# Four seams, an idle start and the last tile of a one-core decoder step: roundings put side by side, matmuls of ones, and a tile that ends in two parts

## The chip, the core and the metric

The kernel runs on one core of one Trainium2 chip. The metric is the device time of one execution in microseconds (us). TensorE (PE) multiplies matrices, VectorE (DVE) and ScalarE (ACT) work element by element on the memories SBUF and PSUM, GpSimd (POOL) gathers and raises to powers, SyncE (SP) issues transfers. Each engine runs its own instructions in the order in which they were written for it, and waits by semaphores for the others.

## The reference

One layer of a hybrid decoder runs for a prompt of 1024 tokens and, beside it, for eight tokens that are being sampled, each with a paged cache of 8192 positions. All numbers are float32.

```python
for l in range(DEPTH):                       # DEPTH = 1
    q, k, v, logf, u, z = mixer_inputs(rmsnorm(xp, g_mix[l]), w_in[l], ...)
    xp = xp + merge_heads(fox_prompt(q, k, v, logf), sgu_prompt(u, z, ...), ..., w_o[l])
    xp = xp + cross_attend(rmsnorm(xp, g_cross[l]), mk, mv, w_cq[l], w_co[l])
    f, conv_p = conv_ffn(rmsnorm(xp, g_ffn[l]), ..., w_up[l], conv_w[l], conv_b[l], w_down[l])
    xp = xp + f
    ...   # the same for the samples xs, with fox_sample over the paged cache
y_prompt = rmsnorm(xp, g_final)
y_sample = rmsnorm(xs, g_final)
```

`rmsnorm(x, g)` is `x * rsqrt(mean(x*x) + eps) * g` over the 1024 columns of a row. The model has 1024 columns, the gated MLP has 2 x 2816.

## The kernel before

**Numbers in two parts.** A float32 operand is split into a high part, rounded to the type fp32r by ACT (`h`), and a remainder `l = x - h` by DVE. A product is three matmuls into one PSUM bank: high times high, high times remainder, remainder times high (`gemm3`, L269 to L274). The weights go through the same split: `wr` is the raw weight, `wh` and `wl` its parts (L235 on ACT, L236 on DVE). `gemm3_late` (L276 to L284) multiplies all that needs only the high part of the rows first (L280, L281) and adds the products with the remainder at the end (L284).

**Stages.** The prompt goes in two halves of 512 rows (`hf` 0 and 1), each four tiles of 128 rows. Each half runs through the mixer, cross-attention and the MLP (`cross`, `ffn`). The samples run as a generator beside it (`decode`): gathers of cache pages by POOL (L1428 for keys, L1489 for values), products of keys and queries on DVE (L1444, in pairs), sums of them (L1448), and small matmuls on PE (L1495). Python code at the end of the kernel mixes the two by a table of costs (`PACE`), and a scheduler with a simulated time line then sets the order of the instructions of each engine. So an edit in one place can move rows of other places.

**A seam** is the change from one stage to the next (`norm_T`, L1106 to L1132). There are four: into cross-attention and into the MLP, for each half. The eight column blocks of the rows have to be transposed on PE, since the next products want columns on the partitions. Tiles 0 and 1 go first, then tiles 2 and 3. Each time four PSUM banks are filled, here called A, B, C and D, with two column blocks of 256 values each (L1124 writes them with four transposes). `split` then takes each block from the bank: ACT rounds it with its gain into `h` (L238), DVE writes the remainder `l` (L239). The two blocks of a bank lie in the same bank, and the program lets one engine at a time read a bank: ACT rounds block 0, DVE takes remainder 0, ACT rounds block 1, DVE takes remainder 1, and each step waits for the one before it. When all eight blocks of the first two tiles are there, `first` begins the next stage's first product with L280, L281 and L284, 256 columns wide.

In the seams into the MLP tiles 2 and 3 come late: `residual` adds the product's last part to the rows (L1015 on DVE) and squares them (L230 on ACT, which writes the row sums with a second instruction), `factor` makes the row's factor (L1031 on ACT, the power L1032 on POOL), and `both` scales tile 2 on ACT (L1044) and tile 3 on DVE (L1045) ahead of the transposes. Eight matmuls that compute nothing needed (`fill`, L1102) run there. In the seams into cross-attention the rows are transposed unscaled, so that only L1015 must be done.

**The start.** PE's first work is L306 (the samples' input product), then L479 to L481 (the prompt's); both wait for weights and rows from HBM. Before that DVE writes constants, `ones` (128x128) among them at L181.

**The end.** In the MLP's last group each tile's product is 15 matmuls of 512 columns, and `residual` follows. `final` (L1355 to L1363) makes the row factor of a tile from the two column halves' sums (L1020, L222 on DVE, the power L223 on POOL), multiplies the rows by factor and gain on DVE (L1361) and writes them with SP's queue (L1362), tile 3 in two halves.

## Time and profile before

| what | value |
|---|---|
| three timed runs | 1788.66, 1794.42 (median), 1794.93 us |
| the profiled execution | 1793.69 us, of which its span 1791.7 us |
| PE | 1735.9 us busy, 97% of the span |
| DVE | 1399.9 us, 78% |
| ACT | 733.5 us, 41% |
| POOL | 488.3 us, 27% |
| moved by DMA | 521.06 MB, mean 291 GB/s |

A row of the time line gives start, duration, engine, line of the kernel, operation, output and inputs by the program's names, shape, and in brackets how long the engine stood idle before it and which instruction ended that. Rows of PE are pipelined: a 512-column matmul's row is about 0.39 us long, while the next one starts 0.23 us after it. In a row of the waits stand the total, the number of times and the longest, in us. In a row of the stretches stand, for each engine, its busy time and its instructions, then the clock that PE was granted (1.00 is full), the DMA engines' share and GB/s.

### The profile page before, as it was taken

The numbers are of one execution on the slowest core, as the hardware profiler recorded it, in microseconds if no ns is written. First come the engines' busy times: TensorE is split into PE (matmuls) and PEld (weight loads), VectorE is DVE, ScalarE is ACT, GpSimd is POOL, SyncE is SP. The second block draws the span as 40 slices with busy tenths as digits, with TensorE's granted clock in tenths as the row PEclk, the third lists the DMA queues.
The fourth block names the chain that finished last, engine by engine and source line by source line (L and its number), as shares of the span: only waits on it lengthen the run. The fifth ranks groups of instructions, "written<-read, shape, count | busy, mean of one in ns | idle before, by whom it ended". The sixth has DMA issues, their size and how long they took to land.

```text
span 1791.7 us, 25124 instructions
## 1 busy us (share of the span) xinstructions
PE 1735.9 (97%) x9653; PEld 1285.7 (72%) x9653; DVE 1399.9 (78%) x1733; ACT 733.5 (41%) x1374; POOL 488.3 (27%) x461
## 2 busy tenths in 40 slices
PE   8999999889999999999999999999999999999997
PEld 5787777655677666767777777766666778768875
DVE  4689658989788986989999999898885549855344
ACT  6332355566643635333333244335353233333232
POOL 1252234443222332333322223433322112102110
PEclk9999999999999999999999999999999999999999
DMA  8786798777697975779788788988879587568982
GB/s 291 297 304 226 294 334 319 259 264 244 254 403 279 363 299 224 282 285 345 290 301 313 291 317 311 376 306 346 320 280 350 214 306 249 191 260 297 359 310 80
DMA packets 157074, 521.06 MB, mean 291 GB/s; under 512 B 20874, under 2 KB 40842, under 8 KB 124186
## 3 DMA queue, kind: packets, MB, share of 16 engines
q0 software_dynamic: 57168, 341.14, 50.0%
q1 hardware_dynamic: 92874, 165.73, 26.5%
q10 hardware_dynamic: 6912, 12.59, 1.9%
q8 instruction: 76, 1.25, 0.3%
q14 instruction: 44, 0.36, 0.1%
HBM read 495.47 MB, written 23.93 MB: 290 GB/s over the span
## 4 chain that ended last, share of the span: by engine, by line
PE 53%; issue 9%; DMA 8%; DVE 6%; ACT 2%; POOL 2%; POOLq 0%; DVEq 0%; ACTq 0%; SPq 0%
DMA kv<-cache_v,io 6%; PE ba L272 6%; PE ba L274 6%; PE ba L273 6%; PE dv L1495 4%; PE bb L272 3%; PE bb L273 3%; PE bb L274 3%; PE ba L1063 1%; DVE s L1448 1%; PE ba L1064 1%; PE ba L1065 1%; PE dv L331 1%; DMA kv<-cache_k,io 1%; PE dv L1774 1%
## 5 line engine op out<-in xcount | busy, mean ns | idle before, releaser
L235 ACT ACTIVATE wh<-wr 128x1024 fp32r<-128x1024 f32 (+2 forms) x220 | 228.6, 1044 | 443.3 <-PE ba L273 142.3
L236 DVE TENSOR_TENSOR wl<-wr,wh 128x1024 fp32r<-128x1024 f32 (+2 forms) x220 | 262.7, 1200 | 165.1 <-PE ba L274 57.4
L1428 POOL DMA_INDIRECT kv<-cache_k,io x128 | 186.9, 1460 | 606.8 <-DVE s L1448 327.2
L1444 DVE TENSOR_TENSOR kv<-kv,d 128x1024 f32<-128x1024 f32 (+1 forms) x156 | 258.0, 1681 | 32.6 <-DMA kv<-cache_k,io 32.6
L1448 DVE TENSOR_REDUCE s<-kv 128x16 f32<-128x1024 f32 (+1 forms) x156 | 258.4, 1672 | 0.0
L1489 POOL DMA_INDIRECT kv<-cache_v,io x128 | 160.8, 1256 | 239.4 <-PE dv L1495 155.2
L272 PE MATMUL ba<-u,wh 128*128 128x512 f32 x528 | 209.3, 397 | 0.0
L274 PE MATMUL ba<-u,wl 128*128 128x512 f32 x528 | 209.0, 396 | 0.0
L273 PE MATMUL ba<-u,wh 128*128 128x512 f32 x528 | 208.5, 395 | 0.5 <-DVE u L239 0.5
L272 PE MATMUL ba<-wh,u 128*128 128x512 f32 (+1 forms) x495 | 186.1, 379 | 0.9 <-ACT u L235 0.9
L273 PE MATMUL ba<-wl,u 128*128 128x512 f32 (+1 forms) x495 | 185.1, 375 | 1.3 <-DVE wl L236 1.3
L274 PE MATMUL ba<-wh,u 128*128 128x512 f32 (+1 forms) x495 | 183.4, 375 | 0.0
L1495 PE MATMUL dv<-kv,s 128*32 128x512 f32 x1024 | 127.1, 598 | 1.6 <-DMA kv<-cache_v,io 1.6
L274 PEld LDWEIGHTS ba<-u,wl 128*128 128x128 f32 x528 | 99.2, 188 | 29.0 <-issue 6.5
L272 PEld LDWEIGHTS ba<-u,wh 128*128 128x128 f32 x528 | 99.3, 188 | 26.4 <-issue 4.8
L273 PEld LDWEIGHTS ba<-u,wh 128*128 128x128 f32 x528 | 99.2, 188 | 25.2 <-issue 2.3
L272 PEld LDWEIGHTS ba<-wh,u 128*128 128x128 f32 x495 | 93.0, 188 | 25.0 <-issue 6.5
L272 PE MATMUL bb<-u,wh 128*128 128x512 f32 x272 | 108.7, 400 | 0.0
L274 PE MATMUL bb<-u,wl 128*128 128x512 f32 x272 | 108.0, 398 | 0.0
L273 PE MATMUL bb<-u,wh 128*128 128x512 f32 x272 | 107.9, 397 | 0.0
L273 PEld LDWEIGHTS ba<-wl,u 128*128 128x128 f32 x495 | 93.0, 188 | 20.1 <-DVE wl L236 1.9
L274 PEld LDWEIGHTS ba<-wh,u 128*128 128x128 f32 x495 | 92.9, 188 | 19.5 <-issue 1.6
(454 smaller groups left out, 3310.6 us busy)
## 6 DMA issues: line engine op xcount, KB each, us to landing
wr<-w_up SPq DMA_DIRECT2D x88, 512.0 KB
kv<-w_up POOLq DMA_DIRECT2D x22, 1024.0 KB
wr<-w_down SPq DMA_DIRECT2D x40, 512.0 KB
kv<-w_down POOLq DMA_DIRECT2D x11, 1024.0 KB
wr<-w_in SPq DMA_DIRECT2D x16, 512.0 KB
wr<-w_o SPq DMA_DIRECT2D x16, 512.0 KB
wr<-w_cq SPq DMA_DIRECT2D x16, 512.0 KB
wr<-w_co SPq DMA_DIRECT2D x16, 512.0 KB
```

What stands on the lines that cost most here:

```text
L235: nc.scalar.activation(h, src, AF.Copy)
L236: nc.vector.tensor_tensor(l, src, h.bitcast(F32), op=ALU.subtract)
L272: mmul(out, sh, mh, start=(i == 0), stop=False)
L273: mmul(out, sh, ml, start=False, stop=False)
L274: mmul(out, sl, mh, start=False, stop=(i == n - 1))
L331: mmul(ps[32 * j : 32 * j + 32, :w], xT[:, k, :] if nk == 8 else xT[:, k * 8 : k * 8 + 32], raw[:, q, j * w : (j + 1) * w], start=(k == 0) ...
L1063: mmul(pss[i], mh[k][:, tb], wh, start=(k == korder[0]), stop=False)
L1428: nc.gpsimd.indirect_dma_start(kv, None, a["cache_k"], off(kidx[:, b, ch : ch + 1]))
L1444: nc.vector.tensor_tensor(kvv[:, i : i + m, :], kvv[:, i : i + m, :], qb.unsqueeze(1).broadcast_to((P, m, 512)), op=ALU.mult)
L1448: nc.vector.tensor_reduce(s[:, ch * 4 + i : ch * 4 + i + m, :].rearrange("p k h -> p (k h)"), kvv[:, i : i + m, :].rearrange("p k (h d) -> ...
L1489: nc.gpsimd.indirect_dma_start(kv, None, a["cache_v"], off(kidx[:, b, ch : ch + 1]))
L1495: mmul(dv[32 * j : 32 * j + 32, :], s[:, ch * 4 : ch * 4 + 4, :].rearrange("p k h -> p (k h)"), kvv[:, j, :], start=(ch == 1), stop=(ch == ...
```

## The change

It has three parts. In `norm_T` ACT now rounds both blocks of a bank one after the other (L1133), and DVE takes both remainders after that (L1135). At the start thirteen matmuls of `ones` by `ones` go into a PSUM tile that nothing reads. The last tile (`last_tile`) is multiplied in two column halves of 256 columns; each half is added (L1311), squared, and its sum taken into the row's mean by ACT (L1313), so that the factor is there after POOL's power (L1316); and `final` multiplies the first 512 columns of tiles 2 and 3 by the gain early (L1398 on DVE), scales them by the factor on ACT (L1399) and writes them apart, tile 3's by ACT's queue (L1400), while DVE does the other 512 columns (L1395).

```diff
+    wm = MS()
+    for _ in range(13):
+        mmul(wm[:, :P], ones, ones, start=True, stop=True)
...
-                    for q in range(2):
-                        k = kk + q
-                        split(tr[:, q * 256 : (q + 1) * 256], hs[k][:, c], ls[k][:, c], scale=gp[:, g0 + k : g0 + k + 1])
+                    gain = [gp[:, g0 + k : g0 + k + 1] for k in (kk, kk + 1)]
+                    src = [tr[:, q * 256 : (q + 1) * 256] for q in range(2)]
+                    for q in range(2):
+                        nc.scalar.activation(hs[kk + q][:, c], src[q], AF.Copy, scale=gain[q])
+                    for q in range(2):
+                        nc.vector.scalar_tensor_tensor(
+                            ls[kk + q][:, c], src[q], gain[q], hs[kk + q][:, c].bitcast(F32), op0=ALU.mult, op1=ALU.subtract
+                        )
...
+        def last_tile(x, sq, pairs):
+            c2 = sm([P, 2], "lsq", 1)
+            part = sm([P, 2], "lpart", 1)
+            r3 = sm([P, 1], "lr", 1)
+            nc.scalar.activation(part[:, 0:1], sq[:, 3, 0:1], AF.Identity, scale=1.0 / D, bias=epsb)
+            for m in range(2):
+                ps = MM()
+                c = slice(m * 256, m * 256 + 256)
+                gemm3(ps[:, :256], [(sh, sl, mh[:, c], ml[:, c]) for sh, sl, mh, ml in pairs])
+                xs_ = x[:, 512 + m * 256 : 768 + m * 256]
+                with tc.high_priority():
+                    nc.vector.tensor_tensor(xs_, ps[:, :256], xs_, op=ALU.add)
+                    ssq_into(c2[:, m : m + 1], xs_)
+                    nc.scalar.activation(
+                        r3 if m else part[:, 1:2], c2[:, m : m + 1], AF.Identity, scale=1.0 / D, bias=part[:, m : m + 1]
+                    )
+            nc.gpsimd.tensor_tensor(r3, r3, mhalf[:, 0:1], op=ALU.pow)
+            lastr.append(r3)
...
+                    if hf and n and i == 3 and f0 + gn == NF:
+                        last_tile(xt[3], sq, [(gh[k][:, tb], gl[k][:, tb], ws[k][0], ws[k][1]) for k in range(gn)])
+                        continue
...
+            if hf and i > 1:
+                r = lastr[0] if i == 3 else rows_rstd(sq, i, i + 1)
+                for n, c in enumerate((slice(0, 512), slice(512, D))):
+                    if n:
+                        nc.vector.scalar_tensor_tensor(xt[i][:, c], xt[i][:, c], r, gf[:, c], op0=ALU.mult, op1=ALU.mult)
+                        nc.sync.dma_start(a["o_y"][rows, c], xt[i][:, c])
+                    else:
+                        nc.vector.tensor_tensor(xt[i][:, c], xt[i][:, c], gf[:, c], op=ALU.mult)
+                        nc.scalar.activation(xt[i][:, c], xt[i][:, c], AF.Copy, scale=r)
+                        (nc.scalar if i == 3 else nc.sync).dma_start(a["o_y"][rows, c], xt[i][:, c])
+                continue
```

The new lines move the old ones down by 3, and by 8, 29, 32 and 44 further on: L238 is now L241 in `split`'s scaled form (the seams no longer use it), L1124 is L1127, L1015 is L1018, L280, L281 and L284 are L283, L284 and L287, L230 is L233, L235 and L236 are L238 and L239, L1444 and L1448 are L1488 and L1492.

Of the order of the instructions three places are shown. The first is ACT at the seam into the MLP of the second half. `u` on the left of a row is the `h` being written, `ba` or `bb` the PSUM bank that it is taken from, `junk` the target of a square, `fac` a row factor. Before:

```order
L238 ACTIVATE u_11036<-ba_11038,gp 128x256 [waits PE_49]
L238 ACTIVATE u_11047<-bb_11049,gp 128x256 [waits PE_49]
L238 ACTIVATE u_11058<-ba_11060,gp 128x256
L238 ACTIVATE u_11036<-ba_11038,gp 128x256 [waits DVE_49]
L238 ACTIVATE u_11069<-ba_11071,gp 128x256
L238 ACTIVATE u_11047<-bb_11049,gp 128x256 [waits DVE_49]
L238 ACTIVATE u_11058<-ba_11060,gp 128x256 [waits DVE_49]
L238 ACTIVATE u_11069<-ba_11071,gp 128x256 [waits DVE_49]
L235 ACTIVATE wh_11391<-wr_11388 128x1024 [waits DMAHW5_49,PE_49]
L230 ACTIVATE junk_11018,sqx_10655<-u_9515 128x512 [waits DVE_49]
L1031 ACTIVATE fac_2074_11023<-sqx_10655,part_10656 128x1 [waits Activation_49]
```

and of the change:

```order
L233 ACTIVATE junk_11032,sqx_10669<-u_9529 128x512 [waits DVE_49]
L1034 ACTIVATE fac_2075_11037<-sqx_10669,part_10670 128x1 [waits Activation_49]
L1133 ACTIVATE u_11050<-ba_11052,gp 128x256 [waits PE_49]
L1133 ACTIVATE u_11050<-ba_11052,gp 128x256
L1133 ACTIVATE u_11061<-bb_11063,gp 128x256 [waits PE_49]
L1133 ACTIVATE u_11061<-bb_11063,gp 128x256
L238 ACTIVATE wh_11405<-wr_11402 128x1024 [waits DMAHW5_49,PE_49]
L1133 ACTIVATE u_11072<-ba_11074,gp 128x256 x2
L1133 ACTIVATE u_11083<-ba_11085,gp 128x256 x2
L233 ACTIVATE junk_11035,sqx_10669<-u_9531 128x512 [waits DVE_49]
L1047 ACTIVATE u_11118<-u_9529,fac_2075_11037 128x512 [waits Pool_49]
```

The waits of ACT for DVE inside the banks are gone; tile 2's square and its factor, which stood behind all eight roundings, now stand ahead of them, and a weight's rounding stands between banks B and C.

The second place is DVE at the seam into cross-attention of the second half, from bank D on. `u_9515` and `u_9517` (now `u_9529` and `u_9531`) are tiles 2 and 3, `kv` the samples' keys, `s` their scores. Before:

```order
L239 SCALAR_TENSOR_TENSOR u_9943<-ba_9944,gp,u_9942 128x256 [waits DMAHW5_49,DMAHW4_49,Activation_49]
L1444 TENSOR_TENSOR kv_9600<-kv_9600,d_1632_8613 128x1024 [waits DMASW5_49]
L1444 TENSOR_TENSOR kv_9600<-kv_9600,d_1632_8613 128x1024
L1015 TENSOR_TENSOR u_9515<-ba_9800,u_9515 128x512 [waits PE_49]
L239 SCALAR_TENSOR_TENSOR u_9943<-ba_9944,gp,u_9942 128x256 [waits Activation_49]
L236 TENSOR_TENSOR wl_9904<-wr_9902,wh_9905 128x1024 [waits DMAHW7_49,PE_49]
L1015 TENSOR_TENSOR u_9517<-ba_9801,u_9517 128x512 [waits PE_49]
```

and of the change:

```order
L1135 SCALAR_TENSOR_TENSOR u_9957<-ba_9958,gp,u_9956 128x256 [waits Activation_49]
L1135 SCALAR_TENSOR_TENSOR u_9957<-ba_9958,gp,u_9956 128x256
L1488 TENSOR_TENSOR kv_9614<-kv_9614,d_1633_8627 128x1024 [waits DMASW5_49]
L1488 TENSOR_TENSOR kv_9614<-kv_9614,d_1633_8627 128x1024
L1492 TENSOR_REDUCE s_8629<-kv_9614 128x16 [waits DVE_49]
L1488 TENSOR_TENSOR kv_9664<-kv_9664,d_1633_8627 128x1024 [waits DMASW6_49]
L1488 TENSOR_TENSOR kv_9664<-kv_9664,d_1633_8627 128x1024
L1018 TENSOR_TENSOR u_9529<-ba_9814,u_9529 128x512 [waits PE_49]
L239 TENSOR_TENSOR wl_9918<-wr_9916,wh_9919 128x1024 [waits DMAHW7_49,PE_49,Activation_49]
L1492 TENSOR_REDUCE s_8629<-kv_9614 128x16 [waits DVE_49]
L1018 TENSOR_TENSOR u_9531<-ba_9815,u_9531 128x512 [waits PE_49]
```

The two remainders now stand together, and tile 2's addition has moved behind a sum and a second pair of key products, tile 3's behind one more sum.

The third place is DVE at the end of the program, from the last product of tile 2 on. `rn2r` and `rn3r` are the factors of tiles 2 and 3 (tile 3's is now `lr`), the last operand of L1361 and L1395 is the gain. Before:

```order
L222 TENSOR_SCALAR rn2r_14800<-rq_2654_14798 128x1 [waits DVE_49]
L1361 SCALAR_TENSOR_TENSOR u_9515<-u_9515,rn2r_14800,u_14782 128x1024 [waits Pool_49]
L1015 TENSOR_TENSOR u_9517<-bb_14762,u_9517 128x512 [waits PE_49]
L1020 TENSOR_TENSOR rq_2656_14805<-sqx_11184 128x1 [waits Activation_49]
L222 TENSOR_SCALAR rn3r_14807<-rq_2656_14805 128x1 [waits DVE_49]
L1361 SCALAR_TENSOR_TENSOR u_9517<-u_9517,rn3r_14807,u_14782 128x512 [waits Pool_49]
```

and of the change:

```order
L1311 TENSOR_TENSOR u_9531<-bb_14780,u_9531 128x256 [waits PE_49]
L225 TENSOR_SCALAR rn2r_14840<-rq_2660_14838 128x1 [waits DVE_49]
L1395 SCALAR_TENSOR_TENSOR u_9529<-u_9529,rn2r_14840,u_14822 128x512 [waits Pool_49]
L1311 TENSOR_TENSOR u_9531<-ba_14800,u_9531 128x256 [waits PE_49]
L1395 SCALAR_TENSOR_TENSOR u_9531<-u_9531,lr_14778,u_14822 128x512 [waits Pool_49]
```

The last tile's addition is in two, its sums are off DVE, and tile 2's scaling on DVE is half as wide.

More of the change, by code (lines that the diff above doesn't have):

```diff
@@ L1357, in final @@
         for i in range(4):
+            rows = slice((hf * 4 + i) * P, (hf * 4 + i + 1) * P)
+            if hf and i > 1:
[9 more added lines that the diff above has]
+                continue
             r = rows_rstd(sq, i, i + 1)
-            rows = slice((hf * 4 + i) * P, (hf * 4 + i + 1) * P)
             for c in (slice(0, 512), slice(512, D)) if i == 3 else (slice(0, D),):
@@ L1365, in build @@
     lastexp = []
+    lastr = []
     last = {}
```

## The prediction

> **What bounds the kernel now.** I read the busy times first, then the waits, and last the time line and the stretches at the places that the change touches.
>
> ```profile
> PE 1735.9 (97%) x9653; PEld 1285.7 (72%) x9653; DVE 1399.9 (78%) x1733; ACT 733.5 (41%) x1374; POOL 488.3 (27%) x461
> ACT u L238 <- DVE u L239: 11.7, 7, 3.7
> ```
>
> TensorE is busy for 97% of the span of 1791.7 us. All its idle time is 1791.7 - 1735.9 = 56 us, and part of that lies at the two ends and in stages that no edit touches. So nothing here can win more than some ten microseconds. The last row is what the first edit aims at: ACT waits 11.7 us in seven places for a remainder. That is ACT's time. What counts is how much of it TensorE waits too.
>
> **The end.**
>
> ```profile
> 1781.75 1.28 DVE L1361 SCALAR_TENSOR_TENSOR u<-u,rn2r,u 128x1024 f32<-128x1024 f32 x1 [0.65 <-POOL rn2r L223]
> 1782.00 0.40 PE L274 MATMUL bb<-wh,u 128*128 128x512 f32 x1
> 1782.95 0.68 DVE L1015 TENSOR_TENSOR u<-bb,u 128x512 f32<-128x512 f32 x1
> 1783.73 0.63 ACT L230 ACTIVATE junk<-u 128x512 bf16<-128x512 f32 x1 [3.26 <-DVE u L1015]
> 1784.27 0.19 ACT L230 ACTIVATION_READ_ACCUMULATOR junk<-u 128x1 f32 x1
> 1784.91 0.54 POOL L223 TENSOR_TENSOR rn3r<-rn3r,mhalf 128x1 f32<-128x1 f32 x1 [3.20 <-DVE rn3r L222]
> 1785.49 1.42 DVE L1361 SCALAR_TENSOR_TENSOR u<-u,rn3r,u 128x512 f32<-128x512 f32 x2 [0.66 <-POOL rn3r L223]
> ```
>
> For the new widths I take rows of the seams, 256 columns on DVE and on ACT, and ACT's sum of one column:
>
> ```profile
> 698.53 0.28 ACT L1031 ACTIVATE fac<-sqx,part 128x1 f32<-128x1 f32 x1
> 1178.49 0.47 DVE L239 SCALAR_TENSOR_TENSOR u<-bb,gp,u 128x256 fp32r<-128x256 f32 x1
> 1178.99 0.47 ACT L238 ACTIVATE u<-bb,gp 128x256 fp32r<-128x256 f32 x1 [2.19 <-DVE u L239]
> ```
>
> TensorE ends at 1782.40 and DVE's last scaling at 1786.91. In the change TensorE ends 0.1 later (thirty narrow matmuls for fifteen). Tile 2's scaling on DVE takes 0.71 in place of 1.28 and ends as TensorE does. Then: second addition 0.47 (a 256-wide row) to 1783.0, square 0.47 + 0.19 to 1783.65, sum by ACT 0.28, POOL 0.54 to 1784.6, and ACT's scaling 0.63 beside DVE's 0.71: 1785.3. That is 1.6 us earlier. The last two transfers now start together, from SP's and from ACT's queue, behind which nothing stands any more; before, 0.7 us lay between them, so sharing costs between nothing and 0.7: I take 0.3. **-1.3** (bounds -1.6 and -0.9). The early multiplications by the gain stand ahead of a weight's remainder some 15 us before the end; if that has no slack, each costs its 0.7 us.
>
> **The seams.** In each bank DVE's first remainder now waits for two roundings, 0.47 more, and the weights' remainders and key products behind it on DVE with it; ACT's second rounding waits for nothing. There are four seams. At the first one (517 to 545 us) TensorE has no gap over 0.6 us; I count 0. The second, into the MLP of half 0:
>
> ```profile
> 696.32 1.33 ACT L1044 ACTIVATE u<-u,fac 128x512 f32<-128x512 f32 x2 [0.68 <-POOL fac L1032]
> 697.71 0.33 PE L1124 MATMUL bb<-cp,u 128*128 128x128 f32 x1 [1.70 <-ACT u L1044]
> 698.17 0.45 ACT L238 ACTIVATE u<-bb,gp 128x256 fp32r<-128x256 f32 x1
> 698.68 0.39 PE L280 MATMUL ba<-u,wh 128*128 128x256 f32 x1 [0.64 <-ACT u L238]
> 700.77 1.84 PE L1102 MATMUL ba<-u 128*128 128x256 f32 x7
> 704.07 0.38 PE L280 MATMUL ba<-u,wh 128*128 128x256 f32 x1
> ```
>
> Bank D's second rounding (698.17) stands behind tile 2's scaling and tile 3's square on ACT, so TensorE waits 1.70 and 0.64 us. In the new order both roundings of D stand ahead of tile 2's square, and L283, L284 and most of L287 run some 3 us earlier. But the path that ends this seam is tile 2's and tile 3's: addition, square, factor, scaling, transposes. On DVE three more remainders now stand ahead of tile 2's addition (3 x 0.47, by the row of 1178.49), so scaled tile 2 comes 1.2 us later, and tile 3's scaling is moved back as far. Against that stands the clock:
>
> ```profile
> 696.16:699.57 3.41, 1.22 (x8) 1.03 (x9) 0.59 (x2) 3.22 (x9) 0.67 (x2) 1.00 1.03 429
> 699.58:702.98 3.40, 3.40 (x18) 3.40 (x17) 2.27 (x7) 0.60 (x2) 1.01 (x1) 0.50 0.64 266
> ```
>
> In the first stretch TensorE was busy for 1.22 of 3.41 us; in the next it was granted half its clock, and the fill and the transposes took twice their time, about 1.7 us more. With the work before the scaling moved into that first stretch TensorE would be busy there for over 2 us, and the half clock may not come. 1.7 less what the later scaling takes: I count **-1.0** (bounds: -3.0 if both waits and the half clock go, +0.6 if the scaling is late and the half clock stays).
>
> The Trainium skill ("TensorE: Matmul & The Clock Gate", section "HAM oscillation — how this bites in real kernels") states the rule as no idle gaps over about 3.4 us. This trace differs: the longest gap here was 1.70 us and the clock fell all the same, with 36% of the stretch busy. By the page's rule the clock could not be at stake at this seam.
>
> The third seam, into cross-attention of half 1:
>
> ```profile
> 1168.58 2.35 DVE L1444 TENSOR_TENSOR kv<-kv,d 128x1024 f32<-128x1024 f32 x2
> 1170.85 0.68 DVE L1015 TENSOR_TENSOR u<-ba,u 128x512 f32<-128x512 f32 x1
> 1171.84 1.22 DVE L236 TENSOR_TENSOR wl<-wr,wh 128x1024 fp32r<-128x1024 f32 x1
> 1172.97 0.69 DVE L1015 TENSOR_TENSOR u<-ba,u 128x512 f32<-128x512 f32 x1
> 1173.57 2.33 DVE L1448 TENSOR_REDUCE s<-kv 128x16 f32<-128x1024 f32 x2
> 1176.21 2.35 DVE L1444 TENSOR_TENSOR kv<-kv,d 128x1024 f32<-128x1024 f32 x2
> 1176.35 0.50 PE L273 MATMUL ba<-u,wh 128*128 128x512 f32 x1 [0.47 <-DVE u L239]
> 1179.52 0.39 PE L280 MATMUL bb<-u,wh 128*128 128x256 f32 x1 [1.70 <-ACT u L238]
> ```
>
> Here the edit fits best. The remainder of 1178.49 stands behind a pair of key products (2.35), ACT's rounding of 1178.99 waits 2.19 for it and TensorE 1.70, with 0.47 before: 2.2 us go if nothing takes their place. Something does. In the new order of DVE tile 2's addition stands behind pair, sum and pair, 2.35 + 1.17 + 2.35 = 5.9 us after D's remainders where it was 2.35, and tile 3's behind an addition, a weight's remainder and one more sum: 0.69 + 1.22 + 1.17. Bank D's transposes have moved up to bank C's in the new order of TensorE, so I let DVE begin the pair 1.1 us earlier, at 1167.5 (my estimate). Tile 2's addition then ends at 1174.1 (before: 1171.5) and tile 3's at 1177.2 (before: 1173.7). By my count of the products ahead of them TensorE comes to tile 2's transposes at about 1171.2 and stands for 2.9 us, does nineteen products of 256 columns (2.3 us) and stands for 0.7 us more: 3.6 in place of 2.2, a loss of 1.4. The walk holds only if DVE is as far behind as before. Between -2.2 and +1.4 I take **0**.
>
> The fourth, into the MLP of half 1:
>
> ```profile
> 1322.01 0.47 ACT L238 ACTIVATE u<-ba,gp 128x256 fp32r<-128x256 f32 x1 [1.10 <-PE ba L1124]
> 1322.98 0.68 DVE L1460 TENSOR_TENSOR s<-s,dec 128x512 f32<-128x512 f32 x1
> 1325.23 0.84 ACT L238 ACTIVATE u<-ba,gp 128x256 fp32r<-128x256 f32 x2 [2.02 <-DVE u L239]
> 1326.43 0.39 PE L280 MATMUL ba<-u,wh 128*128 128x256 f32 x1 [1.05 <-DVE u L239]
> 1327.17 1.05 ACT L235 ACTIVATE wh<-wr 128x1024 fp32r<-128x1024 f32 x1
> 1329.84 1.34 ACT L1044 ACTIVATE u<-u,fac 128x512 f32<-128x512 f32 x2 [0.68 <-POOL fac L1032]
> 1330.61 0.33 PE L1124 MATMUL ba<-cp,u 128*128 128x128 f32 x1 [0.77 <-ACT u L1044]
> ```
>
> ACT's 2.02 and TensorE's 1.05 look like the same gain again. But the new order puts tile 2's square ahead of bank A's roundings, and that waits for tile 2's addition, which waits for DVE to end L1460 (1323.66). Addition 0.68, square 0.63 + 0.19, factor 0.28: A's first rounding starts at 1325.5 where it was 1322.01, and TensorE's first product at 1326.0 instead of 1326.43. Eight roundings at 0.42 and the weight's 1.05 between B and C end at 1329.9, then tile 3's square (0.82) stands ahead of tile 2's scaling: 1330.7 instead of 1329.84. Tile 3's scaling comes out as before. One wait gives way to another: **0** (bounds -2.5, with all the gaps from 1326 to 1333.4 gone, and +0.8).
>
> **The start.**
>
> ```profile
> 0.83 0.17 DVE L181 MEMSET ones<- 128x128 f32 x1 [0.83 <-PEq L2010]
> 7.15 1.92 PE L306 MATMUL ba<-wr,xg 128*32 128x512 f32 x4 [7.15 <-DVE u L239]
> 9.00 0.80 PE L479 MATMUL bb<-wh,u 128*128 128x512 f32 x1
> 10.29 0.40 PE L479 MATMUL bb<-wh,u 128*128 128x512 f32 x1
> ...
> 700.49 0.63 PE L1124 MATMUL ba<-cp,u 128*128 128x128 f32 x2
> ```
>
> TensorE does nothing until 7.15, and L479 took 0.80 us at 9.00 and 0.40 at 10.29: the clock doubled in between. The ones hide wholly in the idle 7 us, so they cost nothing, and delay nothing since the tile is read by nobody. They gain if they bring the full clock earlier, at most half of the 3.0 us from 7.15 to 10.1. Two f32 products of 128 columns took 0.63 us at the half clock, so thirteen end by 1.1 + 13 x 0.32 = 5.2 at the latest, and at least 2 idle us follow. By the second seam's rows a stretch with so little work in it gives the half clock back. I count **-0.1** (bounds: -0.9, half of L306's 1.92 us, and +0.5 if the clock's stretches fall worse).
>
> The Trainium skill (the same page, "Part 1: The HAM clock gate") holds that the full clock comes after a busy window of about 3.4 us and goes after an idle one. By that rule too thirteen matmuls are too few and too early, as an estimate; no run here shows it yet.
>
> **Sum.** -1.0 + 0 + 0 - 0.1 - 1.3 = -2.4 us, against the profiled execution's 1793.69 us: 1791.3 us. That execution is 0.73 us below the median of 1794.42; I leave it at that, since single runs lie 6 us apart. The order moves in most other stages as well: about 1,000 of some 7,000 rows of TensorE stand elsewhere. Their waits can fall either way; from the two 1.7 us gaps above I allow 4 us to each side.
>
> **Rivals.** (1) *The seams give all they show.* DVE is less far behind than in my walk: -3.0 - 2.2 - 2.5 at the seams, -0.5 at the start, -1.5 at the end, 9.7 us together: 1784.0. For it: two waits of ACT of 2 us each with TensorE idle behind them, and a stretch at half the clock. Against it: the new orders of ACT and DVE.
> (2) *Slower.* At the third seam the second pair of key products decides. If TensorE reaches tile 2's transposes before that pair ends, it stands for 3.6 us within 6, under half busy as in the stretch ahead of 699.58, and one or two stretches at half the clock follow, 1.7 us each. With 2 x 1.7 + 1.4 there, +0.8 and +0.6 at the other two, and 1.3 gained at the end, it is +4.9: 1798.6. It decides from the point where tile 2's addition comes over 3 us later than it did.
> (3) *The seams do nothing*, since a TensorE that is 97% busy takes the work up later: only the end's gain is left, 1792.4, and the other rows' moves around it.
>
> **Chances.** My sum 0.40, with a range of its own from 1787 to 1795; (1) 0.25; (2) 0.16; (3) 0.15; the rest (the other stages' order moves more than 4 us) 0.04. The range from 1780 to 1799.5 takes in (1) with its 4 us below, (2) at its price, and leaves out the far ends of both. Half a per cent is 9 us, about what a measurement of this kernel can tell from no change. Faster by more (under 1785.4) is the larger part of (1) and a little of the rest: 0.22. Slower by more (over 1803.4) is the far end of (2): 0.05. Within: 0.73.
>
> **What would show it.** In the profile after: L1133 without a wait for L1135 at all four seams; at 700 us the fill's seven matmuls in under 1 us if the clock held; TensorE's gap ahead of L1127 at the third seam (2.9 us by my walk), and ACT's first L1133 at the fourth at about 1325.5 rather than 1322; L309 still at 1.9 us; DVE's last L1395 some 2.9 us after TensorE's last matmul, where it was 4.5. I am wrong if L309 takes about 1 us and the program moves forward with it, if the third seam has no gap over 1 us, or if the waits of stages without an edit change by more than the seams do.

## The result and the profile after

The change takes 1803.22 us (median of 8 executions, 1799.53 to 1810.58), the kernel before beside it 1794.07 us (8 executions, 1788.66 to 1795.85). The ratio is 1.0060, with a 95% interval from 1.0041 to 1.0078: slower. The profiled execution of the change took 1803.68 us, of which its span is 1801.9 us, 10.2 us more than the span before. First the row of busy times:

```profile
PE 1744.2 (97%) x9694; PEld 1292.4 (72%) x9694; DVE 1398.0 (78%) x1733; ACT 732.5 (41%) x1381; POOL 490.2 (27%) x461
```

TensorE is busy for 8.3 us more than before and idle for 57.7 us in place of 55.8. The start shows why these two do not tell the story yet:

```profile
1.05 5.46 PE L188 MATMUL ms<-ones 128*128 128x128 f32 x26 [1.05 <-DVE mhalf L183]
7.14 1.05 PE L309 MATMUL ba<-wr,xg 128*32 128x512 f32 x4 [0.63 <-DVE u L242]
8.14 0.50 PE L482 MATMUL bb<-wh,u 128*128 128x512 f32 x1
```

The ones are 5.46 us of new "work" in time that was idle. Without them TensorE's busy time is 1738.7, 2.8 us more than before. Its idle time, without the first 7 us, has grown from 48.6 (55.8 - 7.15) to 56.0 (57.7 - 1.05 - 0.63): 7.4 us. These two are the loss. The busy part fits the clock: between the start and the end the trace grants TensorE half its clock for 17.1 us before (five stretches of 3.41 us) and for 23.9 us after (seven), which costs at most half of the difference, 3.4 us. To find the loss's place I cut both traces at the same rounding instructions of the prompt's weights, and compare the lengths (us):

| stretch before | what runs there | before | after | difference | the same order in other kernels |
|---|---|---|---|---|---|
| 0 to 71.3 | start, input products | 71.31 | 69.41 | -1.90 | -1.4 to -0.8 |
| 689.8 to 716.0 | second seam | 26.25 | 22.96 | -3.29 | 0.0 to +1.0 |
| 1164.7 to 1198.2 | third seam | 33.42 | 35.14 | +1.72 | 0.0 to +1.5 |
| 1319.9 to 1347.4 | fourth seam | 27.58 | 28.09 | +0.51 | -1.2 to -1.0 |
| 1766.4 to the end | last tile | 25.29 | 24.37 | -0.92 | 0.0 to +0.2 |
| 309.0 to 490.1 | attention, half 0 | 181.11 | 184.12 | +3.01 | -2.3 to +0.1 |
| 538.0 to 644.9 | end of the first seam, cross-attention, half 0 | 106.88 | 110.67 | +3.79 | +0.4 to +3.7 |
| 1052.5 to 1164.7 | mixer's end and merge, half 1 | 112.26 | 119.77 | +7.51 | -0.3 to +1.4 |
| 1198.2 to 1319.9 | cross-attention, half 1 | 121.70 | 118.43 | -3.27 | -1.1 to +5.9 |
| the five others | | 1085.9 | 1088.9 | +3.03 | -0.5 to +1.3 |

The last column says how far one execution can be trusted. It has the differences from before in kernels of the next section that leave TensorE's order in that stretch as it was before (the last tile alone, four ones, narrow ones, the first seam alone; each left out where its own edit lies). The second seam and the stretches of 309 and 1052 us stand clear of it, those of 538 and 1198 us do not. The first five rows, where the edits are (bar the first seam, which a cut divides), gain 3.9 us together. The others lose 14.1. (Work moves across the cuts too, so that one row is not idle time alone; the sum is the span's 10.2.) Three stretches before, by engine:

```profile
537.98:644.86 106.88, 104.74 (x536) 74.87 (x536) 93.70 (x119) 52.41 (x121) 29.08 (x25) 1.00 0.84 315
689.75:716.00 26.25, 22.82 (x131) 18.63 (x134) 17.20 (x31) 14.93 (x32) 3.06 (x4) 0.93 0.63 252
1102.30:1127.50 25.20, 24.41 (x127) 18.57 (x126) 23.78 (x30) 13.55 (x26) 11.71 (x9) 1.00 0.96 364
```

and the same three after:

```profile
540.22:650.89 110.67, 107.08 (x535) 76.50 (x534) 92.98 (x117) 51.40 (x122) 33.48 (x25) 0.97 0.80 298
695.78:718.74 22.96, 20.05 (x119) 16.91 (x117) 14.73 (x30) 12.26 (x28) 3.06 (x4) 1.00 0.72 288
1108.40:1137.00 28.60, 26.11 (x136) 20.31 (x136) 25.00 (x31) 13.48 (x25) 10.55 (x10) 1.00 0.94 349
```

At the second seam the clock column goes from 0.93 to 1.00: the half clock is gone. In the other two TensorE stands idle for more (2.1 to 3.6, and 0.8 to 2.5 us), and in the first of them the clock falls to 0.97. TensorE's rows with waits in 1100 to 1166 of the change:

```profile
1102.80 0.50 PE L275 MATMUL bb<-wh,u 128*128 128x512 f32 x1 [1.39 <-ACT u L238]
1120.20 1.92 PE L1539 MATMUL dv<-kv,s 128*32 128x512 f32 x16 [2.49 <-DMA kv<-cache_v,io]
1162.79 0.50 PE L1085 MATMUL ba<-wl,u 128*128 128x512 f32 x1 [0.90 <-DVE wl L239]
```

None of these waits is at a line that the diff touches: a rounding into `u` (L238), a weight's remainder (L239), and a samples' product that comes before its gathered values have landed.

### The profile page after: what moved, and what is told of

Its sections match the earlier page's. It is cut to its first block, busy times and chain, and to the rows that moved or that the text cites. A ratio compares the mean times of both kernels' runs of the same rounds, so it can differ in the third digit from the quotient of the medians.

```text
span 1801.9 us, 25253 instructions
## 1 busy us (share of the span) xinstructions
PE 1744.2 (97%) x9694; PEld 1292.4 (72%) x9694; DVE 1398.0 (78%) x1733; ACT 732.5 (41%) x1381; POOL 490.2 (27%) x461
## 3 DMA queue, kind: packets, MB, share of 16 engines
q1 hardware_dynamic: 92874, 165.47, 26.4%
## 4 chain that ended last, share of the span: by engine, by line
PE 58%; DVE 4%; issue 4%; DMA 4%; ACT 2%; POOL 1%; POOLq 0%; DVEq 0%; ACTq 0%; SPq 0%
PE ba L275 8%; PE ba L277 8%; PE ba L276 8%; PE dv L1539 4%; PE bb L275 4%; PE bb L276 4%; PE bb L277 4%; DMA kv<-cache_v,io 1%; PE dv L334 1%; PE dv L1818 1%; DVE kv L1488 1%; DMA kv<-cache_k,io 1%; PE ba L1067 1%; PE ba L1068 1%; PE ba L1066 1%
## 5 line engine op out<-in xcount | busy, mean ns | idle before, releaser
L238 ACT ACTIVATE wh<-wr 128x1024 fp32r<-128x1024 f32 (+2 forms) x220 | 228.7, 1045 | 479.9 <-PE ba L276 143.1
L239 DVE TENSOR_TENSOR wl<-wr,wh 128x1024 fp32r<-128x1024 f32 (+2 forms) x220 | 262.0, 1199 | 164.3 <-PE ba L277 54.1
L1472 POOL DMA_INDIRECT kv<-cache_k,io x128 | 174.6, 1364 | 573.6 <-DVE s L1492 293.7
L1488 DVE TENSOR_TENSOR kv<-kv,d 128x1024 f32<-128x1024 f32 (+1 forms) x156 | 257.9, 1680 | 23.1 <-DMA kv<-cache_k,io 23.1
L1492 DVE TENSOR_REDUCE s<-kv 128x16 f32<-128x1024 f32 (+1 forms) x156 | 258.0, 1673 | 0.0
L1533 POOL DMA_INDIRECT kv<-cache_v,io x128 | 173.3, 1354 | 291.9 <-PE dv L1539 198.5
L275 PE MATMUL ba<-wh,u 128*128 128x512 f32 (+2 forms) x500 | 188.0, 378 | 1.7 <-ACT u L238 1.7
L276 PE MATMUL ba<-wl,u 128*128 128x512 f32 (+2 forms) x500 | 186.9, 374 | 2.2 <-DVE wl L239 2.2
L277 PE MATMUL ba<-wh,u 128*128 128x512 f32 (+2 forms) x500 | 184.4, 374 | 0.0
```

Source lines behind the costliest of these rows:

```text
L238: nc.scalar.activation(h, src, AF.Copy)
L239: nc.vector.tensor_tensor(l, src, h.bitcast(F32), op=ALU.subtract)
L275: mmul(out, sh, mh, start=(i == 0), stop=False)
L276: mmul(out, sh, ml, start=False, stop=False)
L277: mmul(out, sl, mh, start=False, stop=(i == n - 1))
L1472: nc.gpsimd.indirect_dma_start(kv, None, a["cache_k"], off(kidx[:, b, ch : ch + 1]))
```

## The experiments

Rows that have moved are counted below as those outside the runs that both orders of TensorE share (7,057 rows in the order before), so that a row that moves counts at its old place and again at its new one. The change has 3,186 by this count, some 1,600 rows; the prediction's "about 1,000" was too low.

### Each edit alone

Two theories: the seams' edit makes the loss, by the order that it brings, or the ones make it, by the order that their simulated time brings. The first run has the start's three lines and nothing else of the diff (818 rows move, up to 45% of the program):

```diff
+    wm = MS()
+    for _ in range(13):
+        mmul(wm[:, :P], ones, ones, start=True, stop=True)
```

> Only the thirteen matmuls of ones. Theory A (the seams' edit makes the loss by moving the order from the first seam on): L306 takes about 1.05 us in place of 1.92 and the first weights come 1.9 us earlier, the attention of half 0 loses up to 3 us by its moved rows, so between -2 and +2 us against the kernel before; nothing is lost after 1000 us. Theory B (the ones' shift of the order makes the loss): +6 to +12 us, with the stretch from 1050 to 1200 us some 6 us longer.

Measured: 1800.76 us, ratio 1.0053 (1.0034 to 1.0072). Matmuls that nobody reads cost nearly as much as the whole change. In the profile, which has the shortest of the ten executions (1796.85):

```profile
581.03 3.15 PE L1498 MATMUL dv<-kv,s 128*32 128x512 f32 x16 [2.32 <-DMA kv<-cache_v,io]
620.97 3.72 PE L1191 MATMUL ba<-t,u 128*128 128x256 f32 x16 [1.12 <-ACT t L1178]
630.56 1.92 PE L1498 MATMUL dv<-kv,s 128*32 128x512 f32 x16 [1.47 <-DMA kv<-cache_v,io]
```

Some 575 us after the last of the ones TensorE waits twice for gathered values, 3.8 us together, where before it waited 0.3 us in all; this stretch (538 to 645 before) is 7.25 us longer, about twice what an execution in the order of before showed there (+3.7).

The second has the edit of `norm_T` alone (2,628 rows):

```diff
-                    for q in range(2):
-                        k = kk + q
-                        split(tr[:, q * 256 : (q + 1) * 256], ...)
+                    for q in range(2):
+                        nc.scalar.activation(hs[kk + q][:, c], src[q], AF.Copy, scale=gain[q])
+                    for q in range(2):
+                        nc.vector.scalar_tensor_tensor(ls[kk + q][:, c], src[q], gain[q], ...)
```

> Only the roundings put side by side. Theory A: +6 to +12 us; the stretch from 1050 us to the third seam 6 to 8 us longer than before, with gaps of TensorE over 1 us ahead of the third seam, and the second seam some 3 us shorter. Theory B: -5 to 0 us, since the second seam's 3.3 us are gained and the third loses 1 to 2.

Measured: 1800.58 us, 1.0034 (1.0018 to 1.0050). So the seams' edit loses by itself too, and neither theory holds alone. The profiled execution is the shortest of eleven (1792.86 us): second seam -3.28 us, third -2.25, given back at 538 to 645 (+3.73), 1052 to 1102 (+2.51) and elsewhere, so that its span is 0.6 us under that of before. Where the median execution loses its 6 us the profile doesn't show; the theory's 6 to 8 us ahead of the third seam are not there (+1.8).

The third has `last_tile` and the new `final` alone (30 rows, all at the end):

```diff
+                    if hf and n and i == 3 and f0 + gn == NF:
+                        last_tile(xt[3], sq, ...)
+                        continue
```

> Only the last tile in two parts; the order is that of the kernel before up to the last 30 rows of TensorE. Both theories: -0.9 to -1.3 us, all of it after TensorE's last matmul.

Measured: 1791.98 us, 0.9988 (0.9972 to 1.0004); the last stretch is 24.37 us, as in the change.

The fourth has the ones and the last tile (848 rows), with `norm_T` as before:

```diff
+    for _ in range(13):
+        mmul(wm[:, :P], ones, ones, start=True, stop=True)
...
+                        last_tile(xt[3], sq, ...)
```

> All but the seams' edit. Theory A: the ones' result less 1 us, -3 to +1 us against the kernel before and some 10 us under the change. Theory B: +5 to +11 us, about as slow as the change.

Measured: 1803.60 us, 1.0051 (1.0036 to 1.0066). It is as slow as the change, without the seams' edit: the theory that the seams alone make the loss falls.

### Are the ones dear, or the order that they move?

The rival: thirteen matmuls delay something, or their power does, whatever the order. Four ones move no other row; seven bring the same 818 moved rows as thirteen.

```diff
-    for _ in range(13):
+    for _ in range(4):
```

> Four matmuls of ones in place of thirteen: every other row of every engine stands where it stood in the kernel before. Theory A (a moved order costs, whatever moved it): within 1 us of the kernel before, L306 still at about 1.9 us since the ones end by 3 us. Theory B (the ones themselves cost, through the clock or the bank): +2 us or more.

Measured: 1795.64 us, 1.0011 (0.9998 to 1.0025).

```diff
-    for _ in range(13):
+    for _ in range(7):
```

> Seven matmuls of ones: the same moved order as with thirteen, but the ones end at about 4 us, so that the clock should be half again when the data land. Theory A: the loss of the moved order without the start's gain, +8 to +13 us against the kernel before (thirteen gave +9.5 by the ratio), with the stretch from 538 to 645 us 4 us or more longer. Theory B: about half the loss of thirteen, +2 to +6 us.

Measured: 1803.88 us, 1.0068 (1.0047 to 1.0089). Half the ones, the same order, no smaller loss. Ones nearly as long as the change's, but in the order of before, were still missing; ten of 64 columns are that (no other row moves):

```diff
-    for _ in range(13):
-        mmul(wm[:, :P], ones, ones, start=True, stop=True)
+    for _ in range(10):
+        mmul(wm[:, :64], ones, ones[:, :64], start=True, stop=True)
```

> Before, with ten ones matmuls of 64 columns at the start in place of thirteen of 128, and nothing else. They are 20 instructions, each with a weight load; loads took 0.2 us each in the runs with ones, so TensorE should stand in them from 1.05 to about 5.1 us, as long as in the change; yet every other row of the program keeps the place that it had before. Theory A (the loss of the ones is the loss of the order that they move): no loss, 0.9990 to 1.0010 of before, and a first stretch (to 71.3 us) that is up to 1 us shorter if L309 comes at the full clock. Theory B (ones of that duration cost by themselves, by their power or by what they delay): 1.004 to 1.007, as in the kernels with seven and thirteen.

Measured: 1795.75 us, 1.0017 (1.0005 to 1.0030). The time line:

```profile
1.05 4.53 PE L188 MATMUL ms<-ones 128*128 128x64 f32 x20 [1.05 <-DVE mhalf L183]
7.09 1.92 PE L309 MATMUL ba<-wr,xg 128*32 128x512 f32 x4 [1.51 <-DMA wr<-w_in]
```

They hold TensorE for 4.53 us (4.92 for thirteen wide ones alone) and cost a quarter of what the seven wide ones cost. 1.0017 is over what the theory of the moved order allowed (1.0010) and far under that of the ones themselves (1.004). What is left of it, 1 to 5 us, I can't explain; they did not bring the clock up.

### One seam at a time

```diff
+        late_ = g0 == G_FFN
...
+                    if (late_, phase[0][-1]) in [(False, '0')]:
...
+                    else:
```

> The rounding edit at the first seam alone; 148 rows of TensorE move, all near that seam and shortly behind it. Theory A: the loss of the roundings-only run in the stretch from 538 to 645 us (3.7 us) comes from here, so +2 to +5 us. Rival (the second seam's edit moves the order behind it and makes all of the loss): -0.5 to +0.5 us.

Measured: 1799.12 us, 1.0019 (1.0003 to 1.0035), for 148 rows. The second seam alone (2,500 rows, condition `[(True, '0')]`):

> The rounding edit at the second seam alone; about 2,500 rows move, from that seam to the fourth. The seam itself gains 3.3 us as in the change and in the roundings-only run. Theory A: the moved rows behind it give that back and more, +1 to +5 us in all, mostly between 1050 and 1320 us. Rival (only rows close to the edited seam matter): -2 to -4 us.

Measured: 1795.85 us, 1.0012 (0.9993 to 1.0032). Its stretch:

```profile
686.80:709.80 23.00, 20.46 (x122) 17.41 (x121) 14.50 (x30) 12.30 (x28) 3.06 (x4) 1.00 0.73 289
```

Again 3.3 us shorter at the full clock, and the whole no faster: the rival's -2 to -4 us lies outside the interval. The third seam alone (314 rows, condition `[(False, '1')]`):

> Before, with the rounding order changed at the third seam alone (314 rows of TensorE move, between 66% and 78% of the program). My walk in the prediction: a gap of 2.9 us at tile 2's transposes, the stretch from 1164.7 on longer by 1.4 (1.0008). Theory with the fourth-call order of DVE (as in the kernel with all four seams and nothing else, where the pair of products stood ahead of one addition only): stretch shorter by 2.2, ratio 0.9988. Theory A1 (moved rows lose): 1.001 to 1.003, with the loss behind the seam, between 1198 and 1347 us.

Measured: 1792.29 us, 1.0001 (0.9985 to 1.0018), which decides between none of the three theories. DVE's order there and TensorE's only gap:

```profile
1164.93 2.35 DVE L1455 TENSOR_TENSOR kv<-kv,d 128x1024 f32<-128x1024 f32 x2
1167.20 0.68 DVE L1015 TENSOR_TENSOR u<-ba,u 128x512 f32<-128x512 f32 x1
1167.80 1.21 DVE L1459 TENSOR_REDUCE s<-kv 128x16 f32<-128x1024 f32 x1
...
1170.19 0.39 PE L281 MATMUL bb<-u,wl 128*128 128x256 f32 x1 [0.83 <-DVE wl L236]
```

Tile 2's addition (L1015) follows one pair of key products, not two with a sum between them, and the stretch is 3.40 us shorter. The two stretches behind it are 1.5 and 2.5 us longer, the second with the clock at 0.89 (the first lies within what one execution can differ by):

```profile
1192.30:1315.60 123.30, 119.74 (x578) 82.61 (x577) 106.15 (x112) 56.95 (x129) 45.33 (x34) 0.99 0.87 327
1315.60:1345.60 30.00, 25.35 (x151) 18.22 (x150) 22.27 (x40) 14.44 (x28) 6.78 (x8) 0.89 0.73 267
```

### Orders moved without any edit

If moved rows are what costs, they must cost with no edit at all. `PACE`, the table that mixes the samples into the prompt's stages, moves rows when a number in it changes by one or two per cent; the instructions stay the same.

```diff
-PACE = {'p1': 7.0, 'att0': 12.0, ...
+PACE = {'p1': 7.1, 'att0': 12.0, ...
```

> Before, with none of the three edits: the planner's pace for the first phase is 7.1 in place of 7.0. Same instructions, but 2,079 rows of TensorE stand elsewhere, between 11% and 74% of the program. Theory A1 (before's order is one of the better ones, so that nearly any move of so many rows loses): 1.002 to 1.007. Theory A2 (the orders that the ones and the seams bring are bad ones, and a move as such is as likely to gain): between 0.997 and 1.002.

Measured: 1824.54 us, 1.0174 (1.0156 to 1.0193), the slowest kernel of all. Three of TensorE's rows:

```profile
506.16 0.44 PE L872 MATMUL ms<-cp,t 128*128 128x128 f32 x2 [3.80 <-ACT t L861]
...
631.72 3.78 PE L1188 MATMUL bb<-t,u 128*128 128x256 f32 x8 [4.18 <-ACT t L1175]
...
1277.55 2.79 PE L1495 MATMUL dv<-kv,s 128*32 128x512 f32 x12 [5.33 <-DMA kv<-cache_v,io]
```

Between 320 and 1320 us it has five gaps of more than 2 us; before has none (its longest there is 1.72), the change three. Single gaps of this size stand in the order of before too, in other executions (3.72 us with four ones, 2.16 with the narrow ones).

```diff
-PACE = {'p1': 7.0, 'att0': 12.0, ...
+PACE = {'p1': 7.0, 'att0': 12.2, ...
```

> Before, with none of the three edits: the planner's pace for the attention of half 0 is 12.2 in place of 12.0. Same instructions, but 1,681 rows of TensorE stand elsewhere, from 19% of the program on. Theory A1: 1.002 to 1.007. Theory A2: between 0.997 and 1.002, on either side.

Measured: 1806.23 us, 1.0086 (1.0067 to 1.0104). With 11.8 in place of 12.2:

> Before, with none of the three edits: the planner's pace for the attention of half 0 is 11.8 in place of 12.0. Same instructions, 974 rows of TensorE stand elsewhere, from 22% of the program on: about as many as the thirteen ones move (818). Theory A1 (before's order is one of the better ones, nearly any move loses): 1.002 to 1.010. Theory A2 (a move as such is as likely to gain): within 0.997 to 1.002.

Measured: 1806.21 us, 1.0070 (1.0053 to 1.0087). Three of three lose, 7.1 clearly more than the change and the other two at least about as much; 7.1 and 12.2 lie above what the theory of a good order had allowed (1.007).

### The change's edits in three other orders

Two theories: the loss belongs to the order that was drawn, or the edits cost 10 us in any order. Each run is the change with one of the three paces, in the order of the lines:

```diff
-PACE = {'p1': 7.0, 'att0': 12.0, ...
+PACE = {'p1': 7.0, 'att0': 11.8, ...
...
+PACE = {'p1': 7.1, 'att0': 12.0, ...
...
+PACE = {'p1': 7.0, 'att0': 12.2, ...
```

> The change with all three edits, and the pace of the attention of half 0 at 11.8 in place of 12.0. Theory O (the loss belongs to the order that was drawn): another order of the same edits lands elsewhere, more than 4 us from the change's 1.006, to either side. Theory E (the edits cost some 10 us in any order): within 1.004 to 1.008 of before if the pace as such does nothing, and 1.006 behind the kernel with this pace and without the edits in any case.

> The change with all three edits, and the pace of the first phase at 7.1 in place of 7.0, as in the kernel that took 1.0174 without the edits. Theory O: not 1.0174 x 1.006 = 1.0235, but anywhere from 1.000 to 1.020, since the edits draw a new order here too. Theory E: 1.0235, with 1.021 to 1.026.

> The change with all three edits, and the pace of the attention of half 0 at 12.2 in place of 12.0, as in the kernel that took 1.0086 without the edits. Theory O: anywhere from 1.000 to 1.015, more than 4 us from 1.0086 x 1.006 = 1.0147. Theory E: 1.0147, with 1.012 to 1.017.

| pace | without the edits | with the edits | with / without |
|---|---|---|---|
| as before | 1 | 1.0060 (1.0041 to 1.0078) | 1.0060 |
| att0 11.8 | 1.0070 (1.0053 to 1.0087) | 1.0118 (1.0081 to 1.0155) | 1.005 |
| p1 7.1 | 1.0174 (1.0156 to 1.0193) | 1.0157 (1.0128 to 1.0187) | 0.998 |
| att0 12.2 | 1.0086 (1.0067 to 1.0104) | 1.0028 (1.0014 to 1.0041) | 0.994 |

The same edits lose 0.6% in one order and win 0.6% in another. That they cost 10 us in any order is refuted by the last row, whose two intervals lie apart, and by the row of 7.1, which would have had to reach 1.021; 11.8 alone would have fitted it. The second seam of the last kernel, and the mixer's end of half 1:

```profile
697.80:720.70 22.90, 20.39 (x122) 17.40 (x120) 14.49 (x30) 12.25 (x28) 3.06 (x4) 1.00 0.71 288
1054.60:1111.30 56.70, 54.31 (x250) 39.15 (x249) 52.63 (x58) 21.62 (x34) 15.30 (x12) 0.97 0.83 295
```

The first row is the gain that stays with the edit: 22.9 to 23.0 us in five of the six kernels with it (24.2 with the pace of 7.1), against 25.2 to 27.5 us in the twelve kernels without it. All twelve have a stretch at half the clock in this seam; of the six with the edit only that with 7.1 has one. The second is what the order does: 56.7 us, 7 more than before, as with this pace and no edits:

```profile
1058.10:1115.10 57.00, 52.91 (x250) 37.93 (x249) 52.88 (x58) 21.52 (x34) 16.00 (x12) 1.00 0.83 295
```

No version tried is measurably faster than before; the last tile alone, 0.9988 with an interval that reaches 1.0004, is nearest to it.

## Why the prediction was wrong, step by step

**The step that failed: "I allow 4 us to each side" for the other stages' moved order.** I counted it as a mean of nothing with a small spread, and gave 0.04 to its being more. In the profile of the change it was +14.1 us, over three times what its five edited places won. Two of the signs of being wrong that I had named came with it: the stages without an edit changed by more than the seams, and L309 took 1.05 us. That moved order costs is shown by the runs in which rows move without the edits: 1.007 to 1.017 for three paces, 1.005 and 1.007 for ones that leave their 818 moved rows behind, against 1.001 and 1.002 for ones that move none. Of the fourteen kernels above with rows moved elsewhere than in the last tile, none came out faster by more than its interval. The number of moved rows doesn't price it (2,500 for the second seam: 1.0012; 974 for the pace of 11.8: 1.0070); where they lie does. The two 1.7 us gaps from which I took the 4 us were gaps in the order of before, which says little about another order.

**The end, -1.3:** the steps held, one term was mis-sized. The rows of the change:

```profile
1793.29 0.28 PE L277 MATMUL ba<-wh,u 128*128 128x256 f32 x1
...
1795.67 0.75 DVE L1395 SCALAR_TENSOR_TENSOR u<-u,lr,u 128x512 f32<-128x512 f32 x1 [1.52 <-POOL lr L1316]
```

DVE ends at 1796.42, 2.85 us after TensorE, as forecast (2.9). From there to the end of the span it is 5.5 us, where it was 4.8 (1786.91 to 1791.7). That stretch, in which the two last transfers end, grew by 0.7 us: the upper bound that I had given to their sharing, for which I took 0.3. Nothing shown divides it further. So -0.92, and -0.90 to -0.92 in all six kernels with this edit.

**The second seam, -1.0:** right in direction; the measured -3.29 lies just past the bound (-3.0). Both waits and the half clock went. The price that I set against them, a later scaling, was too high: tile 2's addition came 1.2 us later in the stretch, as forecast (2.2 us from its start before, 3.3 after), but ACT's scaling of tile 2 only 0.5 (6.6 to 7.1) and DVE's of tile 3 only 0.3 (9.7 to 10.0). The waits that are left, with ACT's scaling among them:

```profile
700.93 0.39 PE L283 MATMUL ba<-u,wh 128*128 128x256 f32 x1 [0.57 <-ACT u L1133]
...
702.86 1.34 ACT L1047 ACTIVATE u<-u,fac 128x512 f32<-128x512 f32 x2 [0.68 <-POOL fac L1035]
...
703.63 0.33 PE L1127 MATMUL ba<-cp,u 128*128 128x128 f32 x1 [0.76 <-ACT u L1047]
...
706.33 0.87 PE L1127 MATMUL ba<-cp,u 128*128 128x128 f32 x6 [1.20 <-DVE u L1048]
```

**The third seam, 0:** the walk of DVE was right to 0.13 us, in this order. DVE's rows, then TensorE's:

```profile
1178.29 2.35 DVE L1488 TENSOR_TENSOR kv<-kv,d 128x1024 f32<-128x1024 f32 x2
1180.55 1.22 DVE L1492 TENSOR_REDUCE s<-kv 128x16 f32<-128x1024 f32 x1
1181.68 2.35 DVE L1488 TENSOR_TENSOR kv<-kv,d 128x1024 f32<-128x1024 f32 x2
1183.95 0.69 DVE L1018 TENSOR_TENSOR u<-ba,u 128x512 f32<-128x512 f32 x1
```

```profile
1184.69 0.44 PE L1127 MATMUL ba<-cp,u 128*128 128x128 f32 x2 [3.03 <-DVE u L1018]
1185.82 0.39 PE L284 MATMUL bb<-u,wl 128*128 128x256 f32 x1 [0.69 <-DVE wl L239]
```

Forecast were gaps of 2.9 and 0.7; a stretch at half the clock followed, as in the slower rival, which priced two of them. The walk's +1.4 was nearer than the middle: +1.72. That it isn't the edit but the drawn order shows in the other kernels with this edit: -3.40 with the third seam alone, -2.25 with all four seams alone, and -2.59, +1.33 and +4.38 with the three paces. The size itself is no proof, since four ones and the narrow ones have +1.5 and +1.4 here in the order of before; the gap of 3.03 us is.

**The fourth seam, 0:** +0.51, within its bounds, but the execution of before was a poor measure. Its wait of 1.05 us, from which I took the possible gain, isn't in the profile of the last tile alone, with the same order:

```profile
1318.37:1344.94 26.57, 25.06 (x165) 18.91 (x164) 19.97 (x37) 15.97 (x33) 6.63 (x7) 1.00 0.66 238
```

Eight of the kernels without the edit at this seam have 26.4 to 26.6 us here (four others, with rows moved around it, 29.7 to 30.3), all five with it 28.1 to 30.4. Against 26.4 the change lost 1.7 us, past my upper bound of 0.8; whether by the edit or by the moved rows around it is not settled. The stretch comes 10.2 us later than before, and ACT's first rounding, forecast for 1325.5, stands at 1334.88, 0.8 us ahead of that. TensorE's gaps in this stretch sum to 0.5 us instead of 2.7, but more of its work falls into it.

**The start, -0.1:** wrong in its reason. Each of these float32 matmuls is two instructions of 0.21 us on average, so that thirteen end at 6.51 and not at 5.2, and the clock stood over the 0.63 us that follow: L309 took 1.05, not 1.92. By the Trainium skill ("TensorE: Matmul & The Clock Gate", "Part 1: The HAM clock gate") the full clock comes after a busy window of about 3.4 us. The change agrees, with 5.46 us of ones and the full clock behind them; I had used the rule on too short a time. The gain is less than the 1.90 of the table: eight kernels without ones have 69.4 to 70.5 us in this stretch (mean 69.96; before's 71.31 is the longest of all), six with thirteen 69.1 to 69.9 (mean 69.49). It is about 0.5 us.

**The first seam, 0:** not settled. Alone it took 1.0019 (1.0003 to 1.0035) and 3.6 us more from 538 to 645, but four ones, with the order of before, had 3.7 us more in that stretch in their profile too. One execution is too few to tell 3 us in that stage.

**What stays open.** That before's order was one of the better ones is what three paces and the ones point to; how rare it is, they can't say. The paces may also have been set to the best value that was found, so that a step to either side loses for that reason; the ones, which leave them alone, are the cleaner evidence. Which of the moved rows cost most was not tried: the waits shown are for gathers and for tiles that ACT copies out of PSUM (the memory's keys, the attention's output), in stages where the samples' work is mixed in. Part of the loss goes through the clock. The change's eight executions were granted 0.9916 of it on average, the 29 of before beside the first four runs 0.9943; if TensorE had work all the while, that is some 5 of the 9 us, an estimate from these two numbers. The slower executions of one kernel are those with the lower clock as well: of the 29, the ten fastest took 1790.5 us on average at 0.9955, the ten slowest 1799.0 us at 0.9929.

## What to carry to other kernels

Where a scheduler sets the order of the whole program, an edit is two changes: what it does at its place, and a new order everywhere else. Price the second from a null edit (here a pace moved by one or two per cent) before pricing the first, and compare an edit with and without it under more than one order, by medians of several executions: one profile of a stage can differ by 3 to 6 us with the order unchanged. An edit that moves nothing else, like the last tile here, is the only kind here whose profile gain could be added to the time before.

## What the hardware showed besides

**The clock goes by steps of 3.41 us.** In each of the 18 profiles the changes of the granted clock lie whole multiples of 3.413 us apart, and where the steps fall differs from one execution to the next. At the third seam eight profiles have before's order around a wait of 1.70 us. In five, before among them, TensorE was busy for 1.71 to 1.73 us of the step with that wait, and the clock stood. In two, with four ones and with the narrow ones, it was 1.64 to 1.68 us, and the clock fell in the next step. In the eighth a step divides the wait (2.13 us), and the clock stood. Before, then four ones:

```profile
1177.44:1180.85 3.41, 1.71 (x13) 1.36 (x12) 3.41 (x7) 1.33 (x3) 0.00 (x0) 1.00 1.05 403
```

```profile
1178.49:1181.91 3.42, 1.64 (x8) 1.12 (x9) 3.42 (x7) 1.23 (x4) 0.84 (x1) 1.00 1.00 376
1181.91:1185.32 3.41, 3.41 (x13) 3.02 (x14) 3.41 (x7) 0.64 (x2) 0.37 (x1) 0.50 0.47 192
```

Over all 18 profiles the clock fell 92 times, always behind a step with at most 2.25 us busy (66%), and no step at the full clock with less than 1.44 us (42%) kept it. So one and the same order pays for a half clock in one execution and not in the next, which is part of why single profiles differ.

**What brings the clock at the start is not settled.** 14 instructions of 128 columns in 3.36 us brought it, 20 of 64 columns in 4.53 us did not (L309 at 1.92). In both they came 0.23 us or so apart, each with its weight load. But the steps fell otherwise. The one that brought it with seven wide ones was 2.71 us busy, those of the narrow ones 2.54 and 1.99, and 2.80 us of thirteen wide ones (all edits, pace 12.2) did not bring it either; there it came a step later. Seven wide ones, narrow ones, and the change with the pace of 12.2:

```profile
1.70:5.12 3.42, 2.71 (x13) 2.41 (x12) 0.70 (x6) 0.51 (x2) 0.00 (x0) 1.00 0.79 222
```

```profile
0.18:3.59 3.41, 2.54 (x12) 2.54 (x13) 1.37 (x12) 1.49 (x2) 0.44 (x5) 1.00 0.31 64
3.59:7.00 3.41, 1.99 (x10) 1.80 (x9) 0.59 (x1) 1.34 (x3) 0.00 (x0) 1.00 1.01 368
```

```profile
0.44:3.85 3.41, 2.80 (x13) 2.80 (x14) 1.37 (x12) 1.49 (x2) 0.25 (x1) 1.00 0.38 90
```

(The clock column reads 1.00 here because the trace has no entry before the first full clock.) So the narrow ones do not speak against the Trainium skill's rule (same page and part) that the budget is time and not a number of matmuls. And a clock that came early was taken back: with seven ones TensorE stood idle for 2.68 us, L309 still ran at the full clock, and a microsecond later the products fell to half:

```profile
1.05 3.36 PE L188 MATMUL ms<-ones 128*128 128x128 f32 x14 [1.05 <-DVE mhalf L183]
7.09 1.05 PE L309 MATMUL ba<-wr,xg 128*32 128x512 f32 x4 [2.68 <-DMA wr<-w_in]
...
9.17 0.63 PE L482 MATMUL bb<-wh,u 128*128 128x512 f32 x1
```
